# A two-layer decoder trunk: ten low weight parts per layer built by ScalarE and an adding DMA, and queries and keys as one 512-column product

## The chip, the cores and the metric

The kernel runs on one core of one Trainium2 chip. The metric is the device time of one execution in microseconds. The kernel before was run three times; its median is 938.72 us (938.2 to 939.96). With a median of 939 us and runs this close together, about 0.2% (1.9 us) is what a measurement can tell from no change.

## The reference, cut to what is computed

```python
# x: (1, 256, 1024) float32; DEPTH = 2 layers; D_FF = 2816; 4 heads of 64 in each attention
def reference(x, ...):
    for l in range(DEPTH):
        x = x + 0.5 * swiglu(rms_norm(x, ffn1_norm[l]), ffn1_gate[l], ffn1_up[l], ffn1_down[l])
        h = rms_norm(x, mix_norm[l]) @ w_in[l]              # 1024 -> 2304 columns
        u_pool = h[..., :256]                               # pooling
        qm, km, vm = split(h[..., 256:1024], 3)             # block-sparse ("moba") attention
        qd, kd, vd = split(h[..., 1024:1792], 3)            # dilated attention
        u_conv = h[..., 1792:]                              # convolution, 31 taps
        y_pool = pool_mixer(u_pool, pool_w[l], pool_scale[l])
        y_moba = moba_attention(rope(qm), rope(km), vm)
        y_dil  = dilated_attention(rope(qd), rope(kd), vd)
        y_conv = conv_module(u_conv, ...)                   # ends in a layer norm and silu
        x = x + concatenate([y_pool, y_moba, y_dil, y_conv]) @ w_out[l]
        x = x + 0.5 * swiglu(rms_norm(x, ffn2_norm[l]), ffn2_gate[l], ffn2_up[l], ffn2_down[l])
    return rms_norm(x, final_norm)
```

## The kernel before

All matrix products run on TensorE in a 32-bit format of reduced mantissa (fp32r). To keep accuracy, each operand is split in a high part (the value rounded to that format) and a low part (the rest), and each product is the sum of three: high times high, high times low, low times high.

The weights come as a stream of **units** of 128 partitions by up to 2048 columns (1 MB), in the order in which they are used. `prep` loads a unit in two halves of 128x1024: SyncE (SP) issues a DMA into a buffer `raw` (four of them, in turn), ScalarE (ACT) writes the high part `hi` as a copy of `raw`, and VectorE (DVE) writes the low part `lo` as `raw` minus `hi`. `hi` and `lo` are rings of five units, so a unit's buffers are free when the unit five places before it has been used. `raw` is free when both ACT and DVE have read it.

A layer is a first feed-forward part (22 gate/up units `gu`, 16 halves of down units `dn`), the mixing part (9 units `wi` of the input projection, 4 units `wo` of the output projection), and a second feed-forward part. In the mixing part the `wi` units are, in order: conv gate and conv value (`cg`, `ca`), `qd`, `kd`, two for both values `v`, `qm`, `km`, and the pooling columns `pu`. `by_tokens` makes queries and keys: tokens are the stationary side, 256 features of the weights the moving side, so a unit is 48 matmuls of 128x256. The two `v` units hold 512 features per block of 128 inputs and are made by 48 matmuls of 128x512. `rope` scales the product out of PSUM with ACT, rotates with four DVE operations, transposes on TensorE (`tr_qd`, `tr_kd`, ...) and copies the result back with ACT; `scores` and `softmax` follow (`qk_d`, `s_d`, `p_d`), then `pv` transposes the probabilities (`pt_d`), copies them (`pts_d`) and multiplies with `v`. The results are split into `mx` (high by ACT, low by DVE), the operand of the output projection, which takes its four units in the order `W_OUT = (4, 0, 2, 6)`: dilated attention, pooling, moba (`mx` from `pv_m`) and convolution. The 31 convolution taps are mostly DVE operations on `yv`, and a layer norm (`ln`, `rb_ln`) and a silu (`lth`) end them.

Nothing is in the written order: `Plan` records all operations with their dependencies, estimated costs (`rec`) and a due time, and emits them in an order of its own. Every engine then runs its instructions in exactly that order, and waits on semaphores. A changed operation therefore also moves its neighbours.

GpSimd (POOL) only adds the squares for the norms (`acc_f`, `acc_m`).

Of the kernel before, what the change touches and what calls it, by code (L numbers as in the profile page):

```python
# [8 lines left out]
F32 = mybir.dt.float32  # L9
# [7 lines left out]
T = 256  # L17
# [34 lines left out]

ALL, BLOCKS = ((0, KC),), ((0, 4), (4, 6), (6, 7), (7, 8))
W_OUT = (4, 0, 2, 6)

# [15 lines left out]
class View:  # L71
# [21 lines left out]
    def rows(self, n=2):  # L93
        return self._then(lambda t: t.unsqueeze(1).to_broadcast([128, n, T]))

    def heads(self):
        return self._then(lambda t: t.to_broadcast([128, 2, 4, t.shape[3]]))

# [165 lines left out]
def trunk(ctx: ExitStack, tc: tile.TileContext, d):  # L264
# [53 lines left out]
    def dma_act(out, in_):  # L318
        rec("act", 0.47, nc.scalar.dma_start, [out], [], (), {"out": out, "in_": in_}, lat=1.8)

    def store(out, in_, cols):
        rec("sp", max(0.1, cols * 0.00142), nc.sync.dma_start, [], [in_], (), {"out": out, "in_": in_}, lat=0.91)
# [95 lines left out]

    units, output = [], set()
    for l in range(DEPTH):  # L420
        for w in range(2):
            for f in range(FC):
                units.append((d["gu"][l, w, f], 16))
            for m in range(KC):
                for h in range(2):
                    units.append((d["dn"][l, w, m, :, h * HALF:(h + 1) * HALF], FC // 2))
            if w == 0:
                for k in range(9):
                    units.append((d["wi"][l, k], 16))
                for k in range(4):  # L430
                    output.add(len(units))
                    units.append((d["wo"][l, k], 16))
    made = []
# [52 lines left out]
    def prep():  # L486
        n = len(made)
        src, ch = units[n]
        hi = plan.buf(ring, [128, UNIT], F32R, f"hi{n % RING}", f"hi{n}")
        lo = plan.buf(ring, [128, UNIT], F32R, f"lo{n % RING}", f"lo{n}")  # L490
        parts = 2
        plan.lead = LEAD if n in output else 0.0
        where = []
        for i in range(parts):
            a, b = ch * i // parts, ch * (i + 1) // parts
            where += [i] * (b - a)
            a, b = a * 128, b * 128
            raw = plan.buf(ring, [128, UNIT // 2], F32, turn("raw", RAW), f"raw{n}_{i}")[:, :b - a]
            h, o = hi.on(i)[:, a:b], lo.on(i)[:, a:b]
            dma(raw, src[:, a:b], b - a)  # L500
            A(b - a, h, raw, AF.Copy)
            tt(b - a, "tensor_sub", o, raw, h.bitcast(F32))

        plan.lead = 0.0

        def part(c, n=1):

            s = slice(c * 128, (c + n) * 128)
            return hi.on(where[c])[:, s], lo.on(where[c])[:, s]

        made.append(part)
# [212 lines left out]
    def mix(l, nrm, after):  # L724
# [61 lines left out]

        def rope(i, j, nm, col):

            ps = by_tokens(nm)
            q = slot(i, f"{nm}t{l}")  # L790
            for t in range(2):
                A(T, q.on(t)[:, t], ps.on(t)[:, t], AF.Copy, scale=col[:, t:t + 1])
            v = q.rearrange("p t (h e) -> p t h e", h=4)
            a = work("ra", 2, [128, 2, 4, 16], f"ra_{nm}{l}")
            b = work("rb", 2, [128, 2, 4, 16], f"rb_{nm}{l}")
            tt(64, "tensor_mul", b.on(0)[:, :, :, 0:8], v[:, :, :, 8:16], sin_t[:, :, :, 0:8].heads())
            tt(64, "tensor_mul", b.on(1)[:, :, :, 8:16], v[:, :, :, 0:8], sin_t[:, :, :, 8:16].heads())
            tt(128, "tensor_mul", a, v[:, :, :, 0:16], cos_t.heads())
            tt(128, "tensor_add", v[:, :, :, 0:16], a, b)
            ps = bank("qk", 2, [128, 2, T], f"tr_{nm}{l}")  # L800
            for t in range(2):
                for c in range(2):
                    transpose(0.09, ps.on(2 * t + c)[:, c, t * 128:(t + 1) * 128], q[:, t, c * 128:(c + 1) * 128])
            out = slot(j, f"{nm}{l}")
            A(512, out, ps, AF.Copy)
            return out

# [27 lines left out]

        qd = rope(8, 14, "qd", qcol)
        kd = rope(9, 15, "kd", nrm.col)
        pd = [p for c in range(2) for p in scores(qd, kd, c, C_BD, f"d{l}", 16)]


        psv = [bank("mm", 4, [128, 512], f"v{l}{t}") for t in range(2)]
        vt = [flat(slot(20 + t, f"vt{l}{t}")) for t in range(2)]
        sv = [Sum(), Sum()]
        for u in range(2):
            part = take()
            for t in range(2):
                sl = slice(t * 128, (t + 1) * 128)
                for i in range(4):
                    k = u * 4 + i
                    wh, wl = part(4 * i, 4)  # L850
                    xh, xl = nrm.y[k].on(0)[:, 0, sl], nrm.y[k].on(1)[:, 1, sl]
                    sv[t].mm(0.65, psv[t], (xh, wh), (xh, wl), (xl, wh))
        for t in range(2):
# [25 lines left out]

        qm = rope(8, 23, "qm", qcol)  # L880
        km = rope(9, 24, "km", nrm.col)
        pv(pd, 256, 4, 16, f"d{l}")
# [213 lines left out]
```

## Time and profile before

| what | value |
|---|---|
| median of three runs | 938.72 us |
| the profiled execution's own time | 939.43 us |
| its span in the trace | 937.6 us |
| TensorE busy | 924.9 us (99% of the span) |
| VectorE busy | 721.5 us (77%) |
| ScalarE busy | 563.8 us (60%) |
| GpSimd busy | 33.3 us (4%) |
| granted TensorE clock over the span | 0.997 |

The table is to be read with the chain of work that ended last: an engine that is busy for 99% of the span leaves little to gain from the others, except where it waits for them. The span of a profiled execution is 1.83 us shorter than that execution's device time.

### The profile page before, as it was taken

How to read it: one execution, taken by the hardware profiler on the slowest of the kernel's cores; microseconds unless marked ns; L12 is line 12 of the kernel's file. 1: busy time of each engine (PE TensorE's matmuls, PEld its weight loads, DVE VectorE, ACT ScalarE, POOL GpSimd, SP SyncE). 2: the span in 40 equal slices, each digit the busy share in tenths (PEclk: the TensorE clock that was granted, in tenths of full speed). 3: DMA queues.
4: the chain of work that ended last, by engine and by line, in shares of the span. 5: the costliest groups of instructions: out<-in, count | busy, mean ns of one | idle time of the engine just before them, and what ended most of it. 6: DMA issues, size and time to landing. Idle time of an engine off the chain costs nothing.

```text
span 937.6 us, 15074 instructions
## 1 busy us (share of the span) xinstructions
PE 924.9 (99%) x5644; PEld 822.4 (88%) x5644; DVE 721.5 (77%) x1329; ACT 563.8 (60%) x1049; POOL 33.3 (4%) x45
## 2 busy tenths in 40 slices
PE   9999999999999999999999999999999999999996
PEld 8888888898998888888888888888988988888885
DVE  6789976679888988765778887667797888886652
ACT  7776655558576676555546565445667776565540
POOL 0000000100002000000000000011000200000010
PEclk9999999999999999999999999999999999999998
DMA  8856566762164756456765554567512576654641
GB/s 301 280 199 214 171 179 199 232 217 93 35 229 156 249 200 209 127 161 195 251 213 181 180 189 137 166 193 253 187 46 96 197 239 212 221 173 125 187 125 45
DMA packets 55210, 170.18 MB, mean 181 GB/s; under 512 B 6368, under 2 KB 8416, under 8 KB 55136
## 3 DMA queue, kind: packets, MB, share of 16 engines
q1 hardware_dynamic: 54704, 168.92, 55.9%
q8 instruction: 44, 0.72, 0.3%
q10 hardware_dynamic: 432, 0.29, 0.1%
q14 instruction: 30, 0.25, 0.1%
HBM read 168.14 MB, written 1.05 MB: 180 GB/s over the span
## 4 chain that ended last, share of the span: by engine, by line
PE 93%; DVE 3%; DMA 2%; ACT 1%; issue 1%; DVEq 0%; SPq 0%; ACTq 0%
PE mm_gu L368 50%; PE dn L368 26%; PE v L368 2%; PE wo L368 2%; PE pu L368 1%; PE qd L368 1%; PE qm L368 1%; PE kd L368 1%; PE km L368 1%; PE mm_cg L368 1%; PE mm_ca L368 1%; DMA raw<-in_gu_dram 1%; DVE lo L312 1%; DVE y_f L346 1%; DMA x<-in_x_dram 1%
## 5 line engine op out<-in xcount | busy, mean ns | idle before, releaser
L312 DVE TENSOR_TENSOR lo<-raw,hi 128x1024 fp32r<-128x1024 f32 (+3 forms) x365 | 387.7, 1087 | 63.1 <-ACT hi L312 47.3
L312 ACT ACTIVATE hi<-raw 128x1024 fp32r<-128x1024 f32 (+3 forms) x365 | 329.6, 938 | 137.3 <-PE dn L368 54.8
L368 PE MATMUL mm_gu<-y_f,hi 128*128 128x512 f32 x1408 | 332.4, 391 | 0.9 <-DVE y_f L346 0.7
L368 PEld LDWEIGHTS mm_gu<-y_f,hi 128*128 128x128 f32 x1408 | 260.7, 188 | 54.8 <-ACT hi L312 1.8
L368 PEld LDWEIGHTS mm_gu<-y_f,lo 128*128 128x128 f32 x1408 | 176.0, 191 | 4.0
L368 PE MATMUL mm_gu<-y_f,lo 128*128 128x256 f32 x1408 | 178.1, 283 | 0.0
L368 PE MATMUL dn<-h,hi 128*128 128x512 f32 x704 | 169.4, 390 | 0.0
L368 PEld LDWEIGHTS dn<-h,hi 128*128 128x128 f32 x704 | 128.7, 188 | 24.1
L312 DVE TENSOR_TENSOR t<-mm_gu,t 128x256 f32<-128x256 f32 x176 | 73.0, 421 | 49.8 <-ACT t L312 47.1
L368 PEld LDWEIGHTS dn<-h,lo 128*128 128x128 f32 x704 | 91.5, 191 | 4.3
L368 PE MATMUL dn<-h,lo 128*128 128x256 f32 x704 | 92.8, 282 | 0.0
L312 ACT ACTIVATE t<-mm_gu 128x256 f32<-128x256 f32 x176 | 64.3, 375 | 30.0 <-PE mm_gu L368 29.9
L312 ACT ACTIVATE h<-th 128x256 fp32r<-128x256 f32 x88 | 36.4, 417 | 63.2 <-DVE th L312 63.1
L312 DVE TENSOR_TENSOR t<-t,rb_f 128x512 f32<-128x512 f32 x88 | 60.2, 686 | 0.9
L312 ACT ACTIVATE th<-t 128x256 f32<-128x256 f32 x88 | 36.5, 415 | 40.3 <-DVE t L312 28.5
L346 DVE SCALAR_TENSOR_TENSOR x<-dn,x 128x256 f32<-128x256 f32 x64 | 27.0, 422 | 38.8 <-PE dn L368 38.2
L368 PE MATMUL wo<-mx,hi 128*128 128x256 f32 x256 | 48.4, 289 | 1.7 <-DVE mx L312 1.7
L346 DVE SCALAR_TENSOR_TENSOR yv<-hpad,par,yv 128x256 f32<-128x256 f32 x108 | 44.0, 478 | 0.0
L312 DVE TENSOR_TENSOR h<-th,h 128x256 fp32r<-128x256 f32 x88 | 36.8, 420 | 7.6 <-ACT h L312 6.8
L368 PEld LDWEIGHTS wo<-mx,hi 128*128 128x128 f32 x256 | 39.9, 191 | 2.3 <-DVE mx L312 2.2
L312 DVE TENSOR_TENSOR th<-th,t 128x256 f32<-128x256 f32 x88 | 36.8, 419 | 5.5 <-ACT th L312 5.1
L368 PE MATMUL wo<-mx,lo 128*128 128x256 f32 x128 | 36.2, 283 | 0.0
(209 smaller groups left out, 674.4 us busy)
## 6 DMA issues: line engine op xcount, KB each, us to landing
raw<-in_gu_dram SPq DMA_DIRECT2D x170, 512.0 KB, 4.5
raw<-in_dn_dram SPq DMA_DIRECT2D x64, 384.0 KB, 3.6
raw<-in_dn_dram SPq DMA_DIRECT2D x64, 320.0 KB, 3.0
raw<-in_wi_dram SPq DMA_DIRECT2D x36, 512.0 KB, 4.7
raw<-in_wo_dram SPq DMA_DIRECT2D x16, 512.0 KB, 3.9
raw<-in_gu_dram SPq DMA_DIRECT2D x9, 256.0 KB, 5.5
con<-in_con_dram SPq DMA_DIRECT2D x1, 932.0 KB, 7.5
x<-in_x_dram SPq DMA_DIRECT2D x3, 256.0 KB, 5.4
```

The lines of the kernel that those rows point to most:

```text
L312: f(*[val(x) for x in a], **{n: val(x) for n, x in k.items()})
L346: nc.vector.scalar_tensor_tensor(out, in0=a, scalar=scalar, in1=b, op0=op0, op1=op1)
L368: nc.tensor.matmul(val(o), lhsT=val(lhsT), rhs=val(rhs), start=self.i == 0, stop=self.i == self.n - 1, skip_group_check=True)
```

## The change

Two edits. First, for five units of each layer (the ninth `wi` unit, which holds the pooling columns, and the four `wo` units) the low part is no longer a DVE subtraction: ACT writes minus the high part into `lo`, and a DMA issued by GpSimd adds the weights from DRAM onto it. Second, queries and keys of one attention are one product of 512 features: their columns lie side by side in the two units, and the function `wide`, which `v` uses too, runs through both units for both halves of the tokens. `rope` then works on one half of the tokens at a time, queries and keys together.

```diff
@@
+APART = (8,)
@@
+    def dma_add(out, in_):
+        rec("pool", 1.2, nc.gpsimd.dma_start, [out], [], (), {"out": out, "in_": in_, "accum_op": ALU.add}, lat=5.0)
@@
                 for k in range(9):
+                    if k in APART:
+                        apart.add(len(units))
                     units.append((d["wi"][l, k], 16))
                 for k in range(4):
                     output.add(len(units))
+                    apart.add(len(units))
                     units.append((d["wo"][l, k], 16))
@@
             A(b - a, h, raw, AF.Copy)
-            tt(b - a, "tensor_sub", o, raw, h.bitcast(F32))
+            if n in apart:
+                A(b - a, o, h.bitcast(F32), AF.Copy, scale=-1.0)
+                dma_add(o, src[:, a:b])
+            else:
+                tt(b - a, "tensor_sub", o, raw, h.bitcast(F32))
@@
-        def rope(i, j, nm, col):
-
-            ps = by_tokens(nm)
-            q = slot(i, f"{nm}t{l}")
+        def wide(nm):
+
+            ps = [bank("mm", 4, [128, 512], f"{nm}{l}{t}") for t in range(2)]
+            sm = [Sum(), Sum()]
+            for u in range(2):
+                part = take()
+                for t in range(2):
+                    sl = slice(t * 128, (t + 1) * 128)
+                    for i in range(4):
+                        y = nrm.y[u * 4 + i]
+                        wh, wl = part(4 * i, 4)
+                        xh, xl = y.on(0)[:, 0, sl], y.on(1)[:, 1, sl]
+                        sm[t].mm(0.68, ps[t], (xh, wh), (xh, wl), (xl, wh))
+            return ps
+
+        def rope(i, j, nm):
+
+            ps = wide(f"qk{nm}")
+            out = [bank("qk", 2, [128, 2, T], f"tr_{n}{nm}{l}") for n in "qk"]
             for t in range(2):
-                A(T, q.on(t)[:, t], ps.on(t)[:, t], AF.Copy, scale=col[:, t:t + 1])
...
-            for t in range(2):
-                for c in range(2):
-                    transpose(0.09, ps.on(2 * t + c)[:, c, t * 128:(t + 1) * 128], q[:, t, c * 128:(c + 1) * 128])
-            out = slot(j, f"{nm}{l}")
-            A(512, out, ps, AF.Copy)
-            return out
+                qk = flat(slot(i + t, f"qk{nm}t{l}{t}"))
+                for n, col in enumerate((qcol, nrm.col)):
+                    s = slice(n * T, (n + 1) * T)
+                    A(T, qk.on(n)[:, s], ps[t][:, s], AF.Copy, scale=col[:, t:t + 1])
...
+                tt(64, "tensor_mul", b.on(0)[:, :, 0:8], v[:, :, 8:16], sin[:, :, 0:8].to_broadcast([128, 8, 8]))
+                tt(64, "tensor_mul", b.on(1)[:, :, 8:16], v[:, :, 0:8], sin[:, :, 8:16].to_broadcast([128, 8, 8]))
+                tt(128, "tensor_mul", a, v[:, :, 0:16], cos.to_broadcast([128, 8, 16]))
+                tt(128, "tensor_add", v[:, :, 0:16], a, b)
+                for n in range(2):
+                    for c in range(2):
+                        f = n * T + c * 128
+                        transpose(0.09, out[n].on(2 * t + c)[:, c, t * 128:(t + 1) * 128], qk[:, f:f + 128])
+            res = []
+            for n in range(2):
+                res.append(slot(j + n, f"{'qk'[n]}{nm}{l}"))
+                A(512, res[n], out[n], AF.Copy)
+            return res
@@
-        qd = rope(8, 14, "qd", qcol)
-        kd = rope(9, 15, "kd", nrm.col)
+        qd, kd = rope(8, 14, "d")
@@
-        qm = rope(8, 23, "qm", qcol)
-        km = rope(9, 24, "km", nrm.col)
+        qm, km = rope(8, 23, "m")
```

The host code lays the weight columns out to match. The order of SP's DMA issues does not change. At three places the order moves as follows.

TensorE, layer 0, in the values' product behind the dilated queries and keys (`v`: the values; `tr_kd`, `tr_qd`: transposes of the rotated keys and queries; `qk_d`: the scores). Before:

```order
L368 MATMUL v_2391<-hi_2098,y_m_3_1844 128x512
L312 MATMUL tr_kd_2422<-ident,kdt_2395 128x128 x4
L368 MATMUL v_2427<-hi_2098,y_m_0_1624 128x512
L368 MATMUL v_2427<-lo_2125,y_m_0_1624 128x512
L368 MATMUL v_2427<-hi_2098,y_m_0_1624 128x512
L368 MATMUL v_2427<-hi_2098,y_m_1_1696 128x512
L368 MATMUL v_2427<-lo_2125,y_m_1_1696 128x512
L368 MATMUL v_2427<-hi_2098,y_m_1_1696 128x512
L380 MATMUL qk_d_2437<-kd_2431,qd_2346 128x128
```

and with the change:

```order
L311 MATMUL tr_qd_2325<-ident,qkdt_2328 128x128 x2
L311 MATMUL tr_kd_2330<-ident,qkdt_2328 128x128 x2
L370 MATMUL v_2333<-hi_2098,y_m_3_1844 128x512
L370 MATMUL v_2333<-lo_2125,y_m_3_1844 128x512
L370 MATMUL v_2333<-hi_2098,y_m_3_1844 128x512
L370 MATMUL v_2368<-hi_2098,y_m_0_1624 128x512
L370 MATMUL v_2368<-lo_2125,y_m_0_1624 128x512
L370 MATMUL v_2368<-hi_2098,y_m_0_1624 128x512
L382 MATMUL qk_d_2374<-kd_2366,qd_2361 128x128
```

Between the last transposes and the scores there are six matmuls of `v` in both; before, those transposes were of the keys alone, now they are of both.

ScalarE, layer 0, from the layer norm's squares (`lsq`) to the high parts of the moba result (`mx` from `pv_m`). Before:

```order
L312 ACTIVATE lsq_2993<-yv_2354 128x512
L312 ACTIVATE hi_3008<-raw_0_2843 128x1024
L312 ACTIVATE hi_3008<-raw_1_2919 128x1024
L312 ACTIVATE hi_3021<-raw_0_2949 128x1024
L312 ACTIVATE hi_3021<-raw_1_2988 128x1024
L312 ACTIVATE mx_3052<-pv_m_2998 128x256
L312 ACTIVATE mx_3059<-pv_m_3003 128x256
L312 ACTIVATE rb_ln_3071<-ln_3015 128x256
```

and with the change:

```order
L311 ACTIVATE lsq_2910<-yv_2338 128x512
L311 ACTIVATE lo_2925<-hi_2701 128x1024 x2
L311 ACTIVATE hi_2937<-raw_0_2611 128x1024
L311 ACTIVATE hi_2937<-raw_1_2639 128x1024
L311 ACTIVATE lo_2969<-hi_2937 128x1024 x2
L311 ACTIVATE rb_ln_2995<-ln_2931 128x256
L311 ACTIVATE mx_3000<-pv_m_2915 128x256
L311 ACTIVATE mx_3007<-pv_m_2920 128x256
```

The third output unit (`lo_2925`) now has its negation here, behind it comes the fourth (`hi_2937`, `lo_2969`); six operations of 128x1024 instead of four, and `rb_ln`, stand ahead of `mx`.

VectorE at the same place, from the end of the layer norm's iteration (`y_ln`) to the low parts of the moba result. Before:

```order
L346 SCALAR_TENSOR_TENSOR y_ln_3028<-a_ln_3033,y_ln_3028 128x2
L312 TENSOR_TENSOR lo_3013<-raw_1_2919,hi_3008 128x1024
L312 TENSOR_TENSOR lo_3076<-raw_0_2949,hi_3021 128x1024
L312 TENSOR_TENSOR yv_2354<-yv_2354,rb_ln_3071 128x512
L312 TENSOR_TENSOR lo_3076<-raw_1_2988,hi_3021 128x1024
L312 TENSOR_TENSOR mx_3052<-pv_m_2998,mx_3052 128x256
L312 TENSOR_TENSOR mx_3059<-pv_m_3003,mx_3059 128x256
```

and with the change:

```order
L348 SCALAR_TENSOR_TENSOR y_ln_2944<-a_ln_2946,y_ln_2944 128x2
L311 TENSOR_TENSOR yv_2338<-yv_2338,rb_ln_2995 128x512
L311 TENSOR_TENSOR mx_3000<-pv_m_2915,mx_3000 128x256
L311 TENSOR_TENSOR mx_3007<-pv_m_2920,mx_3007 128x256
L348 SCALAR_TENSOR_TENSOR yv_2338<-lth_3025,yv_2338 128x512
```

The three low parts that stood between the iteration and `mx` are gone from VectorE.

## Rows read from the trace of the kernel before

**Rows 1.** The page: busy time of each engine, then the chain's shares by engine
```profile
PE 924.9 (99%) x5644; PEld 822.4 (88%) x5644; DVE 721.5 (77%) x1329; ACT 563.8 (60%) x1049; POOL 33.3 (4%) x45
...
PE 93%; DVE 3%; DMA 2%; ACT 1%; issue 1%; DVEq 0%; SPq 0%; ACTq 0%
```

**Rows 2.** Waits of TensorE: what waited for what, us in total, times, longest
```profile
PE wo L368 <- DVE mx L312: 1.7, 2, 0.9
...
PE mm_gu L368 <- DVE y_f L346: 0.7, 2, 0.4
PE st_f L312 <- DVE y_f L346: 0.4, 1, 0.4
```

**Rows 3.** Timeline of TensorE: start, us, operation, xcount; narrow keys, then wide values
```profile
213.95 0.28 PE L368 MATMUL kd<-lo,y_m 128*128 128x256 f32 x1
...
214.67 0.28 PE L368 MATMUL kd<-lo,y_m 128*128 128x256 f32 x1
...
215.15 0.40 PE L368 MATMUL v<-lo,y_m 128*128 128x512 f32 x1
...
217.21 0.39 PE L368 MATMUL v<-lo,y_m 128*128 128x512 f32 x1
```

**Rows 4.** Timeline of TensorE: the same values' product, later
```profile
223.22 0.39 PE L368 MATMUL v<-lo,y_m 128*128 128x512 f32 x1
...
225.30 0.39 PE L368 MATMUL v<-lo,y_m 128*128 128x512 f32 x1
...
225.98 0.39 PE L368 MATMUL v<-lo,y_m 128*128 128x512 f32 x1
...
228.02 0.39 PE L368 MATMUL v<-lo,y_m 128*128 128x512 f32 x1
```

**Rows 5.** Timeline: ScalarE's copy of the keys, TensorE's first scores
```profile
218.30 0.60 ACT L312 ACTIVATE kd<-tr_kd 128x512 f32<-128x512 f32 x1
...
219.59 0.93 PE L380 MATMUL qk_d<-kd,qd 64*128 64x128 f32 x8
```

**Rows 6.** Timeline of TensorE: the third output unit, which holds the moba result
```profile
269.50 0.28 PE L368 MATMUL wo<-mx,hi 128*128 128x256 f32 x1
270.65 0.38 PE L368 MATMUL wo<-mx,hi 128*128 128x256 f32 x1 [0.87 <-DVE mx L312]
```

**Rows 7.** Timeline of ScalarE ahead of that unit
```profile
261.38 0.62 ACT L312 ACTIVATE lsq<-yv 128x512 f32<-128x512 f32 x1
261.91 3.89 ACT L312 ACTIVATE hi<-raw 128x1024 fp32r<-128x1024 f32 x4
...
267.17 0.39 ACT L312 ACTIVATE rb_ln<-ln 128x256 f32<-128x256 f32 x1 [0.83 <-PE ln L312]
```

**Rows 8.** Timeline of VectorE ahead of that unit
```profile
268.44 0.68 DVE L312 TENSOR_TENSOR yv<-yv,rb_ln 128x512 f32<-128x512 f32 x1
269.04 1.22 DVE L312 TENSOR_TENSOR lo<-raw,hi 128x1024 fp32r<-128x1024 f32 x1
270.18 0.75 DVE L312 TENSOR_TENSOR mx<-pv_m,mx 128x256 fp32r<-128x256 f32 x2
```

**Rows 9.** Groups by line and shape, 191 to 285 us: xcount, busy us, mean ns
```profile
L312 DVE TENSOR_TENSOR lo<-raw,hi 128x1024 fp32r<-128x1024 f32 x23 | 27.7, 1220 | 2.4 <-ACT hi L312 2.4
...
L312 ACT ACTIVATE hi<-raw 128x1024 fp32r<-128x1024 f32 x24 | 24.3, 1055 | 6.6 <-issue 3.1 <-DMA raw<-in_gu_dram 2.8 <-PE dn L368 0.5
```

**Rows 10.** SP's nine loads of 512 KB, 262 to 285 us: issue to landing
```profile
DMA to landing us min/median/max: 3.2/4.9/6.1
```

**Rows 11.** Stretches: us, busy PE, PEld, DVE, ACT, POOL, clock, DMA share, GB/s
```profile
234.00:240.00 6.00, 6.00 (x53) 6.00 (x52) 5.54 (x17) 1.44 (x3) 0.00 (x0) 1.00 0.00 0
240.00:247.00 7.00, 7.00 (x65) 6.58 (x66) 6.83 (x20) 3.46 (x8) 0.00 (x0) 1.00 0.00 0
...
270.00:276.00 6.00, 5.35 (x44) 5.35 (x45) 5.49 (x9) 4.27 (x7) 0.00 (x0) 1.00 0.81 274
```

**Rows 12.** The chain that ended last, layer 0, into the second feed-forward part
```profile
290.81 6.21 DMA raw<-in_gu_dram
297.05 1.06 ACT hi L312
```

More of the change, by code (lines that the diff above doesn't have):

```diff
@@ L94, in rows @@
         return self._then(lambda t: t.unsqueeze(1).to_broadcast([128, n, T]))
-    def heads(self):
-        return self._then(lambda t: t.to_broadcast([128, 2, 4, t.shape[3]]))
     def to_broadcast(self, shape):
@@ L416, in trunk @@
         Sum().mm(0.4, warm[:, 0:128], (mean_w, mean_w))
-    units, output = [], set()
+    units, output, apart = [], set(), set()
     for l in range(DEPTH):
@@ L785, in by_tokens @@
             return ps
-        def rope(i, j, nm, col):
-            ps = by_tokens(nm)
-            q = slot(i, f"{nm}t{l}")
-            for t in range(2):
-                A(T, q.on(t)[:, t], ps.on(t)[:, t], AF.Copy, scale=col[:, t:t + 1])
[L793 to L800, printed above, removed]
-            for t in range(2):
-                for c in range(2):
-                    transpose(0.09, ps.on(2 * t + c)[:, c, t * 128:(t + 1) * 128], q[:, t, c * 128:(c + 1) * 128])
-            out = slot(j, f"{nm}{l}")
-            A(512, out, ps, AF.Copy)
-            return out
+        def wide(nm):
[11 more added lines that the diff above has]
+            return ps
@@ new lines, in rope @@
+        def rope(i, j, nm):
+            ps = wide(f"qk{nm}")
+            out = [bank("qk", 2, [128, 2, T], f"tr_{n}{nm}{l}") for n in "qk"]
+            for t in range(2):
+                qk = flat(slot(i + t, f"qk{nm}t{l}{t}"))
+                for n, col in enumerate((qcol, nrm.col)):
+                    s = slice(n * T, (n + 1) * T)
+                    A(T, qk.on(n)[:, s], ps[t][:, s], AF.Copy, scale=col[:, t:t + 1])
+                v = qk.rearrange("p (h e) -> p h e", h=8)
+                a = work("ra", 2, [128, 8, 16], f"ra_{nm}{l}{t}")
+                b = work("rb", 2, [128, 8, 16], f"rb_{nm}{l}{t}")
+                sin, cos = sin_t[:, t], cos_t[:, t]
+                tt(64, "tensor_mul", b.on(0)[:, :, 0:8], v[:, :, 8:16], sin[:, :, 0:8].to_broadcast([128, 8, 8]))
[11 more added lines that the diff above has]
+            return res
@@ L834, in softmax @@
             return p
-        qd = rope(8, 14, "qd", qcol)
-        kd = rope(9, 15, "kd", nrm.col)
+        qd, kd = rope(8, 14, "d")
         pd = [p for c in range(2) for p in scores(qd, kd, c, C_BD, f"d{l}", 16)]
-        psv = [bank("mm", 4, [128, 512], f"v{l}{t}") for t in range(2)]
+        psv = wide("v")
         vt = [flat(slot(20 + t, f"vt{l}{t}")) for t in range(2)]
[L843 to L852, printed above, removed]
         for t in range(2):
@@ L1053 @@
     plw = np.zeros((DEPTH, 128, 2, 128), f32)
-    cols = [16, 17, 14, 15, 8, 9, 10, 11, 2, 3, 4, 5, 0, 1]
+    cols = [16, 17, 14, 15, 0, 1]
     for l in range(DEPTH):
@@ L1060 @@
         win = I["w_in"][l].reshape(KC, 128, 18, 128)
-        wi[l, [0, 1, 2, 3, 6, 7, 8]] = (win[:, :, cols].reshape(KC, 128, 7, 2, 128).transpose(2, 1, 0, 3, 4)
-                                        .reshape(7, 128, UNIT))
-        wi[l, 4:6] = win[:, :, [6, 7, 12, 13]].reshape(2, 4, 128, 512).transpose(0, 2, 1, 3).reshape(2, 128, UNIT)
+        wi[l, [0, 1, 8]] = (win[:, :, cols].reshape(KC, 128, 3, 2, 128).transpose(2, 1, 0, 3, 4)
+                            .reshape(3, 128, UNIT))
+        for u, four in ((2, [8, 9, 10, 11]), (4, [6, 7, 12, 13]), (6, [2, 3, 4, 5])):
+            wi[l, u:u + 2] = win[:, :, four].reshape(2, 4, 128, 512).transpose(0, 2, 1, 3).reshape(2, 128, UNIT)
         wot = I["w_out"][l].reshape(KC, 128, KC, 128)
```

## The prediction

> **What bounds the kernel now.** I read the page first, then the waits of TensorE, then the timeline at each place where it waits. TensorE is busy for 924.9 of 937.6 us and carries 93% of the chain that ended last [rows 1]. So only two things can shorten this kernel by more than a trifle: fewer or cheaper columns on TensorE, or one of its few waits taken away. VectorE at 77% and ScalarE at 60% [rows 1] hide behind it nearly everywhere, and what an edit takes from them is worth only what TensorE waited for it. Those waits are few [rows 2]: 1.7 us in two pieces, one per layer, for the low part of the moba result (`mx`) in the third output unit, 0.7 us in two pieces for `y_f` and 0.4 us for the row transposes of the norm behind the output projection. One of the 0.7 us's two pieces lies at the kernel's start, which the change doesn't touch; the other, 0.4 us, and the last one are in layer 0 behind the mixing part. So 1.75 + 0.8 = 2.55 us is all that a relieved VectorE can give here.
>
> **The change part by part.**
>
> *Wide queries and keys.* Removed per attention: 96 matmuls of 128x256; added: 48 of 128x512. Columns are the same, so the difference is what each instruction costs beside its columns. The narrow ones start every 0.120 us: six between 213.95 and 214.67 [rows 3]. The wide ones of `v`, which have the very form of the new ones, start every 0.229 us: nine between 215.15 and 217.21 [rows 3]. A pair of narrow ones costs 0.240, so each wide one saves 0.011 us, 48 of them 0.53 us, and four attentions (two in each layer) 2.1 us. The later stretches of the same product bound it: nine in 2.08 us give 0.2311 and 1.7 us, nine in 2.04 us give 0.2267 and 2.55 us [rows 4]. All of it is on TensorE and so on the path. I take 2.1, the stretch nearest to the place of the new products. ScalarE's copies out of PSUM and VectorE's four rotations keep number and size, as do the transposes.
>
> *The new order around the scores.* Before, queries were transposed and copied long before the keys. Now the last transposes bring both, and ScalarE has two copies of 128x512 to make where it had one, under the same six matmuls of `v` (6 x 0.229 = 1.37 us). Before, the keys' copy ended at 218.90 and the scores began at 219.59 [rows 5]: 0.69 us to spare. The second copy takes a further 0.5 to 0.6 of it, if ScalarE is free at once. That leaves about 0.1 us, and nothing if a convolution tap stands ahead of the copies. Bounds: 0, if all fits; if both attentions in both layers lose half a copy more, 4 x 0.35 = 1.4 us. I take +0.4.
>
> *VectorE's share of the low parts.* Removed: ten subtractions in each layer at 1.22 us, 24.4 us in all [rows 9]. Added on ScalarE: as many negations, priced as the copy of the same shape, 1.055 us or 0.97 apart when four run in a row (3.89/4) [rows 7, 9], some 20 us. Both are beside TensorE's work except at one place. In the third output unit TensorE stood from its first matmul at 269.50 until 270.65 [rows 6], because the low part of `mx` came at 270.18 on VectorE behind a low part of 1.22 us at 269.04 [rows 8]. Both layers do this. With the change three of those low parts are no longer there, but ScalarE has more ahead of `mx`: from the end of `lsq` at about 261.9 [rows 7] six operations of 0.97 end at 267.7, `rb_ln` (0.3) at 268.0, the first high part of `mx` at 268.35. VectorE multiplies `yv` meanwhile (0.6, to 268.6) and has the first low part at 269.0; with some 0.2 us to TensorE it comes at 269.2, where the second matmul of the unit would start at 269.62. So the wait goes, with 0.4 us to spare: the price that ScalarE pays stays under cover, but just so. Bounds 0 and 1.75 us; I take 1.5. (All of these times move earlier together by what the wide products save ahead of them; distances stay.)
>
> *The feed-forward part behind it, layer 0.* The 0.4 us wait for the norm's row hangs on a load that was issued at 290.81 and took 6.2 us [rows 12]: `raw` had come free late, since a VectorE that ran behind had still to read it. For the ten halves `raw` is now free when ScalarE has read it, so the next loads leave earlier, into a DMA that stood idle from 234 to 247 us [rows 11]. Between 0 and 0.8 us; I take half, 0.4.
>
> *The adding DMA.* Ten in a layer, 512 KB each, issued by GpSimd, whose queue holds nothing else there; behind them are only its additions for the next norm, which wait for the finished output projection anyway. They use DRAM reads that the DMA has room for [rows 11], but the low part now exists only when the transfer has landed. No row shows a transfer from GpSimd, nor one that adds. Where TensorE needs the data late this doesn't matter: the pooling unit and the first two output units are negated far ahead. The third output unit is the tight one. Its first negation ends at 261.9 + 0.97 = 262.9, its low part is wanted by the unit's third matmul at 269.74: 6.9 us. The fourth unit's negations end near 266.7 and 267.7 and are wanted at 275.3 and 275.6: 8 us or more. The nearest rows are SP's loads of the same size in this stretch: 3.2 to 6.1 us, median 4.9 [rows 10]. With ScalarE's signal and GpSimd's issue ahead of it, 5 to 7 us would fit. The upper bound is two such transfers in one, since the destination is read as well: 9.8 by the median, 12.2 by the longest. I take about 7, at the edge, and put +0.2 us a layer on it: 0.4.
>
> The Trainium skill, DMA: Bandwidth & Descriptors, section Anatomy of one DMA — SWDGE (gpsimd) path, gives 2.0 us plus the bytes over 436 GB/s for a plain transfer from this queue; as an estimate that is 3.2 us for 512 KB, and by it the term would be nothing. SP's row is longer than that for a plain load, and no run here shows GpSimd's.
>
> *Sum,* against the profiled execution: 939.43 - 2.1 + 0.4 - 1.5 - 0.4 + 0.4 = 936.2 us. That execution was 0.7 us over the median of the three runs, 938.72, so against the median the same sum of -3.2 gives **935.5 us**.
>
> **The rivals.**
>
> *1. The additions land late, and the third output unit waits longer than before.* At 9.8 us from the negation's end the low part comes at 272.7, TensorE waits 2.95 instead of 0.87 us, 2.1 more in each layer: 4.2 - 2.1 (wide) = +2.1, 940.8 us. At 12.2 it is 275.1, a wait of 5.3, 4.5 more in each layer: 8.9 - 2.1 = +6.8, 945.5 us. The fourth unit then finds its own landed. It decides from 8.8 us on (the wide products' gain is spent) and is slower by more than 0.2% from 9.7 us. For it: two reads for one write, and a DMA that was 81% busy at 270 to 276 [rows 11]. Against it: the loads that filled it then leave earlier now. The Trainium skill, Collectives: The Full Stack, section The bandwidth ceiling: the fold count and why AG ≠ RS ≠ AR, has this as a rule: a transfer that adds reads two sources through one ring and ran at half the rate of a copy there. No run here shows it yet. Chance 0.17; a landing between 8 and 9.7 us, which ends within 0.2% (about 938.5), 0.08.
>
> *2. The products gain and the new order takes it back.* If `rope`'s copies are late in all four attentions (+1.4), the `mx` wait stays by half (ScalarE's six operations late by the 0.4 us that are to spare, and more), and layer 0's waits stay: -2.1 + 1.4 - 0.9 = -1.6, about 937.1 us, no measurable change. For it: margins of 0.1 and 0.4 us. Chance 0.16.
>
> *3. The wide product is no cheaper than two narrow ones.* If the new ones start every 0.24 us, only the waits are left: -1.5, 937.2 us. Against it stand all three stretches of `v`. Chance 0.02.
>
> **How the numbers follow.** Forecast, with everything between a gain of 1.9 and of 5.1 us (all of the wide products at their best and all waits): 0.57. Faster by over 0.2% (1.9 us, about what a measurement of this kernel can tell from no change) is that case alone, 0.57. Within 0.2%: 0.16 + 0.02 + 0.08 = 0.26. Slower: 0.17. The low end of the range is 938.72 - 5.1 = 933.6, less half a microsecond for the spread of the runs, 933.1; the high end goes into rival 1 as far as a landing of about 10.5 us (+3.4), 942.1, and leaves out some 0.1 above.
>
> **What the profile of the changed kernel would show.** Step 1: the product of queries and keys at 0.227 to 0.231 us from start to start, four products some 2 us shorter in all. Step 2: no wait of TensorE ahead of `qk_d` and `qk_m` above 0.4 us. Step 3: no wait of the output product for `mx`. Step 4: no wait for `y_f` in layer 0 behind the mixing part. Step 5: GpSimd's transfers at 5 to 7 us from issue to landing; a wait of the output product for a DMA, and its length, is the measure of rival 1. The prediction is wrong if that wait is over 2 us a layer, or if the queries' and keys' copies have become what the scores wait for.

## The result: 950.38 us, and the profile after

The changed kernel takes 950.38 us (median of four runs, 948.25 to 951.54) against 938.8 us for the kernel before beside it: a ratio of 1.0118 with a 95% interval of 1.0106 to 1.0131. It is slower by some 11 us where 3 us of gain were forecast. The profiled execution took 950.8 us, its span is 948.9 us.

The page of the changed kernel: busy time of each engine, the chain's shares, the DMA queues (packets, MB, share of 16 engines' span; q1 carries SP's loads, q0 GpSimd's transfers), and three kinds of DMA with their median time to landing:

```profile
PE 926.3 (98%) x5452; PEld 816.0 (86%) x5452; DVE 699.4 (74%) x1309; ACT 582.4 (61%) x1069; POOL 49.4 (5%) x65
...
q1 hardware_dynamic: 54704, 168.92, 55.0%
q0 software_dynamic: 2880, 10.49, 5.9%
...
PE 86%; DMA 8%; ACT 3%; DVE 1%; issue 1%; ACTq 0%; DVEq 0%; SPq 0%
...
raw<-in_wo_dram SPq DMA_DIRECT2D x16, 512.0 KB, 8.7
lo<-in_wo_dram POOLq DMA_DIRECT2D x16, 512.0 KB, 11.9
```

Against [rows 1], VectorE lost 22 us of work and ScalarE took on 19, as reckoned, and TensorE's share of the chain fell from 93 to 86%: what came in is DMA, 8% where it was 2. The waits of TensorE in the changed kernel (us in total, times, longest):

```profile
PE wo L370 <- DMA lo<-in_wo_dram: 9.9, 4, 2.7
PE st_f L311 <- DVE y_f L348: 1.6, 1, 1.6
...
PE pt_d L311 <- ACT pts_d L311: 0.8, 1, 0.8
```

The `mx` waits of [rows 2] are gone, and layer 0's waits for `y_f` behind the mixing part too. In their place the output product waits 9.9 us for adding transfers. (The 1.6 us for `y_f` lie in the first feed-forward part, which the change doesn't touch: in the profiles of the sixteen kernels told of here the queries' product of layer 0 starts between 202.6 and 203.9 us, here at 203.9. The 0.8 us for `pts_d` lie in layer 1.) The places, in TensorE's timeline of layer 0 (start, us):

```profile
270.32 0.28 PE L370 MATMUL wo<-mx,lo 128*128 128x256 f32 x1
...
274.10 0.58 PE L370 MATMUL wo<-mx,lo 128*128 128x256 f32 x1 [2.54 <-DMA lo<-in_wo_dram]
...
277.46 0.31 PE L370 MATMUL wo<-mx,lo 128*128 128x256 f32 x1
...
282.64 0.38 PE L370 MATMUL wo<-mx,lo 128*128 128x256 f32 x1 [2.13 <-DMA lo<-in_wo_dram]
```

The third unit runs through its first half and stops at the second, the fourth does the same. GpSimd issues the four transfers of these units at 263.47, 264.4, 267.26 and 268.2; the time from issue to landing is 5.3, 9.6, 10.6 and 14.4 us (GpSimd's timeline):

```profile
263.47 1.81 POOL L311 DMA_DIRECT2D lo<-in_wo_dram  x2 [17.14 <-ACT lo L311]
267.26 1.81 POOL L311 DMA_DIRECT2D lo<-in_wo_dram  x2 [1.98 <-PE ln L311]
```

and, in the view of the tile, the shortest, median and longest of each pair:

```profile
DMA to landing us min/median/max: 5.3/7.5/9.6
...
DMA to landing us min/median/max: 10.6/12.5/14.4
```

So they land at 268.8, 274.0, 277.9 and 282.6: one by one, 3.9 to 5.2 us apart, and two of the four are the ends of TensorE's two waits. Stretches of the changed kernel (columns as in [rows 11]):

```profile
234.00:240.00 6.00, 6.00 (x28) 4.75 (x27) 5.97 (x18) 5.29 (x8) 2.36 (x3) 1.00 0.95 214
240.00:247.00 7.00, 7.00 (x62) 6.56 (x63) 6.83 (x20) 6.87 (x12) 1.73 (x2) 1.00 1.05 273
...
270.00:276.00 6.00, 3.46 (x23) 3.26 (x22) 4.30 (x6) 4.22 (x7) 0.00 (x0) 0.84 1.02 242
```

The DMA, idle here before (0.00 in both of the first two stretches of [rows 11]), is now full: the first six transfers fill it from 234 us on, the last four meet SP's loads for the feed-forward part.

Where the time lies, from the starts of the first and last matmuls of the tiles in TensorE's timeline, us for layer 0 / layer 1 (two of the kernels below beside it):

| kernel | queries' product to end of `v` | on to the last `wo` | on to the last gate/up |
|---|---|---|---|
| before | 25.6 / 25.6 | 53.8 / 53.8 | 124.6 / 123.1 |
| changed | 25.0 / 25.0 | 58.9 / 61.7 | 123.0 / 122.9 |
| changed, transfers not issued | 25.0 / 25.0 | 52.1 / 52.1 | 123.0 / 122.9 |
| changed, first six transfers only | 25.0 / 25.0 | 52.1 / 52.3 | 123.2 / 123.0 |

The two outer stages gain, 0.6 us a layer in the first, 1.7 in layer 0's feed-forward part; the stage with the transfers loses 5.1 and 7.9 us.

### The profile page after: what moved, and what is told of

Read it like the earlier page. It is cut to its first block, busy times and chain, and to the rows that moved or that the text cites. A ratio compares the mean times of both kernels' runs of the same rounds, so it can differ in the third digit from the quotient of the medians.

```text
span 948.9 us, 14742 instructions
## 1 busy us (share of the span) xinstructions
PE 926.3 (98%) x5452; PEld 816.0 (86%) x5452; DVE 699.4 (74%) x1309; ACT 582.4 (61%) x1069; POOL 49.4 (5%) x65
## 3 DMA queue, kind: packets, MB, share of 16 engines
q0 software_dynamic: 2880, 10.49, 5.9%
## 4 chain that ended last, share of the span: by engine, by line
PE 86%; DMA 8%; ACT 3%; DVE 1%; issue 1%; ACTq 0%; DVEq 0%; SPq 0%
PE mm_gu L370 47%; PE dn L370 26%; DMA lo<-in_wo_dram 3%; DMA raw<-in_gu_dram 3%; PE wo L370 2%; PE qkd L370 2%; PE v L370 1%; PE mm_cg L370 1%; PE pu L370 1%; PE mm_ca L370 1%; PE qkm L370 1%; ACT hi L311 1%; DMA x<-in_x_dram 1%; DMA raw<-in_wo_dram 1%; ACT lo L311 1%
## 5 line engine op out<-in xcount | busy, mean ns | idle before, releaser
L311 DVE TENSOR_TENSOR lo<-raw,hi 128x1024 fp32r<-128x1024 f32 (+3 forms) x345 | 363.0, 1077 | 65.8 <-ACT hi L311 50.2
L370 PE MATMUL wo<-mx,hi 128*128 128x256 f32 x256 | 51.6, 302 | 0.0
L370 PE MATMUL wo<-mx,lo 128*128 128x256 f32 x128 | 38.7, 303 | 9.9 <-DMA lo<-in_wo_dram 9.9
L370 PEld LDWEIGHTS wo<-mx,hi 128*128 128x128 f32 x256 | 43.0, 207 | 0.3 <-issue 0.3
```

The lines of the kernel that those rows point to most:

```text
L311: f(*[val(x) for x in a], **{n: val(x) for n, x in k.items()})
L370: nc.tensor.matmul(val(o), lhsT=val(lhsT), rhs=val(rhs), start=self.i == 0, stop=self.i == self.n - 1, skip_group_check=True)
```

## Experiments

### What of the transfers costs

Three kernels leave all engines in the changed kernel's order and change the transfers alone. None at all:

```diff
-        rec("pool", 1.2, nc.gpsimd.dma_start, [out], [], (), {"out": out, "in_": in_, "accum_op": ALU.add}, lat=5.0)
+        rec("pool", 1.2, lambda **k: None, [out], [], (), {"out": out, "in_": in_}, lat=5.0)
```

> The changed kernel, every engine in the same order, but the ten adding transfers of a layer are not issued (so in five units of each layer the low part holds minus the high part, and the weights are not added). Theory A, the loss of 11.6 us is the transfers alone, late for the output product and crowding the DMA: 934 to 937 us, no wait of the output product for a DMA, no loads over 7 us there. Theory C, ScalarE's twenty negations and the new order around the moba result cost it: 945 us or more, with a wait of the output product for ScalarE or VectorE. Between the two, 940 to 944, each has a part.

Measured 934.05 us, ratio 0.995 (0.9935 to 0.9964). Theory A: the whole loss is the transfers', and a gain of 5.1 us stands behind it. The only wait of TensorE that this profile shows between the program's first and last steps stands at 8.6 us, in the first feed-forward part; from there to the last norm there is none:

```profile
PE mm_gu L370 <- DVE lo L311: 0.5, 1, 0.5
```

Then the same transfers as plain copies:

```diff
-{"out": out, "in_": in_, "accum_op": ALU.add}
+{"out": out, "in_": in_}
```

> The changed kernel, every engine in the same order, but GpSimd's transfers write the weights over the low part where the changed kernel adds them onto it (so in five units of each layer the low part holds the whole weight). Theory A1, it is the adding (the destination is read too): a transfer alone lands in about 3 to 5 us, a line of four moves at 2 to 3 us apiece, the wait of the output product falls from 9.9 us to under 2, and the time is 936 to 941 us. Theory D, it is GpSimd's queue, whatever it carries: a line still moves at 4 us or more apiece, 947 to 952 us.

Measured 936.72 us (0.9979, 0.997 to 0.9988), waits of the output product for a DMA 2.1 us. So of the 16.3 us between the kernels with and without transfers, 13.7 go with the adding and 2.7 with the copying. And the adding transfer with half the columns:

```diff
-{"out": out, "in_": in_, "accum_op": ALU.add}
+{"out": out[:, 0:512], "in_": in_[:, 0:512], "accum_op": ALU.add}
```

> The changed kernel, every engine in the same order, each of the ten adding transfers of a layer carrying the first 512 of its 1024 columns (the other half of those low parts holds minus the high part, the weights are not added there). Theory bytes, the line goes by what is moved: 2 to 2.5 us from landing to landing where it was 4.3 to 5.3, the waits of the output product for a DMA fall from 9.9 us to under 1, 934 to 937 us. Theory count, each transfer costs by itself: 4 us and more from landing to landing, waits of 6 us or more, 944 us or more.

Measured 936.11 us (0.9961, 0.9948 to 0.9973), waits 1.8 us; the time is theory bytes', the waits a little more than it said. What the two have in common stands in the queue line of the page, of the plain copies:

```profile
q0 software_dynamic: 2880, 10.49, 3.2%
```

and of the half adding transfers:

```profile
q0 software_dynamic: 2880, 5.24, 3.3%
```

Adding 5.24 MB keeps the DMA engines about as long as copying 10.49 MB; adding 10.49 MB took 5.9% (the page of the changed kernel above), 1.84 times the plain copies. The number of transfers is the same in all three. The line is not bytes alone, though: in layer 0 of all three kernels the second of the four late transfers lands 5.2 to 5.7 us behind the first, and two loads of SP are issued in between (265.1 and 266.0 us in the changed kernel); the third and fourth follow 2.5 and 1.2 us later as plain copies, 3.9 and 4.7 as additions.

### Which of the ten

Only the third and fourth output unit by adding transfer, the other six low parts by VectorE again (`APART` empty, and ahead of the output units' `apart.add` a condition):

```diff
+                    if k in (2, 3):
                         apart.add(len(units))
```

> The changed kernel with only the third and fourth output unit by negation and adding transfer (four transfers in a layer where it had ten, the other six low parts by VectorE again). Theory A, the line of four begun at 263 is the loss: the waits for a DMA stay at 8 to 11 us, and with what VectorE loses 948 to 954 us. Theory E, the six early transfers cause it: those waits fall under 4 us, 940 to 946 us.

Measured 956.72 us (1.0194, 1.017 to 1.0218), waits for a DMA 9.8 us: theory A in the waits, and 2.7 us above its range in the time, with waits for VectorE and ScalarE beside them (2.4 us of `pt_m` for `yv`, 1.7 of `psp` for `pl`) that the wide product alone has too (next section). Four transfers with none ahead of them form the same line. GpSimd's timeline, and TensorE's where it waits:

```profile
266.22 1.01 POOL L311 DMA_DIRECT2D lo<-in_wo_dram  x1 [79.56 <-DVE yv L311]
267.91 0.87 POOL L311 DMA_DIRECT2D lo<-in_wo_dram  x1 [0.68 <-PE ln L370]
270.74 1.81 POOL L311 DMA_DIRECT2D lo<-in_wo_dram  x2 [1.96 <-ACT lo L311]
...
277.45 0.39 PE L370 MATMUL wo<-mx,lo 128*128 128x256 f32 x1 [2.12 <-DMA lo<-in_wo_dram]
...
285.96 0.58 PE L370 MATMUL wo<-mx,lo 128*128 128x256 f32 x1 [3.57 <-DMA lo<-in_wo_dram]
```

Its transfers landed 7.4, 9.5, 10.5 and 14.2 us after issue. And the complement, the pooling unit and the first two output units by transfer, the last two by VectorE:

```diff
+                    if k in (0, 1):
                         apart.add(len(units))
```

> The changed kernel with the pooling unit and the first two output units by adding transfer (six in a layer, none late for its use), the third and fourth output unit by VectorE's subtraction. The complement of the kernel with these two alone (956.7 us). If only the late four hurt: no wait of the output product for a DMA, some of VectorE's wait ahead of the moba result back (1.7 us), 935 to 940 us. If the six early ones hurt by filling the DMA: 942 us or more, with waits for hi or raw.

Measured 934.92 us, ratio 0.9954 (0.9939 to 0.9968): faster than both kernels. Its six transfers took 8.4 to 14.8 us each and nobody waited for one; the line is there, and it is done before its use. VectorE, with three units' subtractions less, has the other four low parts and `mx` in time; TensorE's only waits between the program's first and last steps are 1.2 us of gate/up for a high part and 0.3 for a norm, all in the first feed-forward part, which the change doesn't touch.

### Each edit alone

The wide product alone (no unit is put in `apart`):

```diff
-APART = (8,)
+APART = ()
...
+                    if k in ():
                         apart.add(len(units))
```

> Queries and keys as one product of 512 features, all low parts by VectorE as before. Theory A, the loss is the transfers' and the wide product gains as forecast: 936 to 938 us (-2.1 for the product, 0 to +0.4 for the order around the scores; the wait for the low part of the moba result stays, 1.7 us). Theory B, the wide product's order costs more than it gains (rival 2 taken further): 940 us or more, with waits ahead of qk_d and qk_m.

And the transfers alone, the first edit made in the kernel before:

```diff
+            if n in apart:
+                A(b - a, o, h.bitcast(F32), AF.Copy, scale=-1.0)
+                dma_add(o, src[:, a:b])
+            else:
                 tt(b - a, "tensor_sub", o, raw, h.bitcast(F32))
```

> The kernel before with the ten low parts of a layer by negation and adding transfer, narrow products kept. Theory A: the loss of the changed kernel and the 2 us that the wide product gives, 951 to 954 us, waits of the output product for a DMA of 8 to 11 us in all. Theory B, the two edits together cause the loss (the shorter products in front leave the transfers less time): 940 to 946 us.

Measured 945.8 us (1.0081, 1.0064 to 1.0097) and 939.63 us (1.0009, 1.0 to 1.0018). Both expectations of theory A fell. Theory B of the first has the time (940 us or more) and not the place, that of the second is missed by 0.4 us. The wide product alone loses 6.7 us, though its own stage is 0.6 us a layer shorter. The transfers alone neither lose nor gain clear of the noise, and no wait for them is in that profile (an execution of 941.58 us, the slowest of ten): its stage up to the last `wo` is 1 us a layer shorter than before, and its gate/up part some 2 us a layer longer (with 1.9 us of waits for `y_f` there, and in layer 0 the granted clock at 0.52 from 284.0 to 287.5 us). The waits of the kernel with the wide product alone:

```profile
PE pt_m L311 <- DVE yv L348: 2.4, 2, 1.2
PE psp L370 <- ACT pl L311: 1.7, 2, 0.8
PE ln L370 <- DVE lsq L311: 1.6, 2, 1.2
PE wo L370 <- DVE lo L311: 1.6, 2, 0.8
PE mm_gu L370 <- ACT hi L311: 1.6, 3, 0.9
```

None stands ahead of the scores. They come from further up. A stretch (columns as in [rows 11]) of the kernel before:

```profile
216.00:229.00 13.00, 13.00 (x70) 9.91 (x69) 11.78 (x41) 11.53 (x31) 0.00 (x0) 1.00 0.29 103
```

and of the wide product alone:

```profile
216.00:229.00 13.00, 13.00 (x67) 9.87 (x66) 9.15 (x37) 12.68 (x37) 0.00 (x0) 1.00 0.01 3
```

The DMA stands still for 13 us and VectorE is idle for 3.9 of them, while ScalarE has no time left. What it does not do there is the pooling unit's high parts. ScalarE's timeline in the kernel before:

```profile
216.24 2.00 ACT L312 ACTIVATE hi<-raw 128x1024 fp32r<-128x1024 f32 x2
```

and with the wide product alone:

```profile
228.42 1.05 ACT L311 ACTIVATE hi<-raw 128x1024 fp32r<-128x1024 f32 x1
```

Before, ScalarE made five of the convolution's gates (`gt`) while TensorE was still busy with the keys, and was through with the sixth at 216.4 us. With queries and keys together it waits 0.7 and 1.9 us for the halves of the product, copies both out of PSUM at 212.1 and 214.9 us, makes all six gates behind that, and the planner puts the pooling unit behind the dilated softmax, 12 us later. Until ScalarE has read that unit `raw` isn't free, so SP can't load, and VectorE has its low parts to make later, in the middle of the convolution's taps. In the changed kernel the same shift moves the transfers: the first leaves at 231.7 us, with the narrow product at 220.1, and the third unit's leave at 263.5 instead of 243.6 and 245.8 (GpSimd's timelines). That was tested by moving the unit's due time, in the kernel with the wide product alone and in the changed kernel (`ninth` holds the pooling unit's number; in the changed kernel `apart` stands there, which picks the same unit, since the others in it are in `output`):

```diff
-        plan.lead = LEAD if n in output else 0.0
+        plan.lead = LEAD if n in output else 30.0 if n in ninth else 0.0
```

> Queries and keys as one product, all low parts by VectorE (945.8 us so), and the pooling unit's preparation due 30 us earlier. Theory A2, the loss of that kernel too is the displaced preparation (weights stand still from 216 to 229 us, convolution and low parts pile up on VectorE behind it): 936 to 940 us, its waits of 7 to 8 us for yv, pl, lsq and lo mostly gone. Theory V, VectorE lacks the time in the wide order wherever that unit stands: 943 to 947 us.

> The changed kernel, with the due time of the pooling unit's preparation 30 us earlier in the planner, so that ScalarE makes its two high parts and negations ahead of the dilated softmax, as the kernel with narrow products and adding transfers does, and the units behind it follow some 11 us earlier. Theory A2, the wide product pushes ScalarE's preparation of the pooling unit behind the softmax, and the transfers are late by that shift alone: 935 to 938 us, waits of the output product for a DMA under 1.5 us in all. Theory A, ten adding transfers of 4.5 us are too slow for this stage wherever they begin: 945 us or more.

Measured 939.43 us (0.9999, 0.999 to 1.0008), 6.4 us back, and 940.65 us (1.0018, 1.0008 to 1.0027), 9.7 us back; the high parts stand at 215.0 and 215.4 us. In the second no wait for a DMA is left at the output product, with the third unit's transfers leaving at 249.31:

```profile
219.74 1.92 POOL L311 DMA_DIRECT2D lo<-in_wi_dram  x2 [32.15 <-ACT lo L311]
...
249.31 1.80 POOL L311 DMA_DIRECT2D lo<-in_wo_dram  x2 [6.00 <-ACT lo L311]
```

Theory A2 holds for the shift, but the second kernel is 2.7 us above its range. Whether the transfers cost those:

> The changed kernel with the pooling unit prepared early (940.65 us so), every engine in that order, and the ten adding transfers of a layer not issued (five units' low parts hold minus the high part; the weights are not added). Theory A2 with E: the 6 us by which that kernel stays behind the one without transfers (934.05) are still the transfers', which fill the DMA and delay the loads of the next feed-forward part: 933 to 936 us, no wait of mm_gu for hi or y_f over 0.5 us. Theory O: they are the order's: 938 to 941 us.

Measured 938.62 us (0.9997, 0.9989 to 1.0006): theory O. In that order the transfers cost 2.0 us, no more; that it stays 4.6 us behind the same work in the changed kernel's order is the order's (in the two profiled executions, whose spans are 6.0 us apart, 1.1 and 0.8 us up to the last `wo` and 2.1 and 1.8 in the gate/up part). Which of its places costs that was not tried. The three orders side by side, us:

| order | low parts by VectorE | negated, no transfer | negated, with transfers |
|---|---|---|---|
| narrow products | 939.1 | not run | 939.6 |
| wide | 945.8 | 934.05 | 950.4 |
| wide, pooling unit early | 939.4 | 938.6 | 940.65 |

The second and third columns of a row are one order with and without the transfers, which cost 16.3 and 2.0 us. For the first column the planner had made the order anew, so the 11.8 us (second row) and 0.8 (third) between it and the next are the worth of the subtractions and of that order together.

### Other choices

The planner told that an adding transfer takes 20 us, which moves the third unit's negations ahead of `lsq`:

```diff
-"accum_op": ALU.add}, lat=5.0)
+"accum_op": ALU.add}, lat=20.0)
```

> The changed kernel, with an adding transfer taken as 20 us long in the planner where it was 5: the third output unit's two negations move from behind the layer norm's squares to some 8 us ahead of them, all else nearly as it was. Theory A, four transfers in one line at 4 to 5 us each, begun at 263: the line is now two and two, no wait of the output product for a DMA above 0.5 us, 934 to 938 us. Theory E, the six transfers before them fill the DMA and that delays what follows: a wait of 4 us or more stays, 941 us or more.

Measured 953.42 us (1.0145, 1.0128 to 1.0163). No wait of the output product for a DMA, as theory A has it, and yet slower: the order around it moved as well, and TensorE waits for `pts_d` (3.5 us), `yv` (2.5), `mn_m` (1.6) and `y_f` (3.4) instead. As a test of the time it is inconclusive.

In the order with the pooling unit early, the transfers for the first two output units alone, for the first three, and for the pooling unit and the first three (the three lines, one for each kernel; the first two with `APART` empty):

```diff
+                    if k in (0, 1):
...
+                    if k in (0, 1, 2):
...
+                    if k in (0, 1, 2):
```

> Wide queries and keys, the pooling unit prepared early with VectorE's subtraction, and negation and adding transfer for the first two output units alone (four transfers in a layer, from about 233 to 246 us, where the DMA stood idle, VectorE was full and ScalarE had room). If the transfers cost only where they meet the loads or a late use: 935 to 938 us, no wait of the output product for a DMA, psp and y_f waits about halved from 3.4 us. If any adding transfers cost by themselves: 940 us or more.

> The same with the third output unit too (six transfers in a layer). Its two transfers start near 246 and land near 256 to 260, ten microseconds ahead of their use: if only lateness and meeting the loads matter, 934.5 to 938 us and VectorE's wait ahead of the moba result gone. If crowding starts with the loads of the fourth unit: 0.5 to 2 us slower than with two.

> The changed kernel with the pooling unit early (940.65 us so) and the fourth output unit's two transfers, issued at 265 to 267 us into the loads of the feed-forward part, replaced by VectorE's subtractions. If those two are what is left of the transfers' price there (about 2 us): 937 to 939 us, no wait of mm_gu for hi. If the order is what is left: 940 to 942 us.

Measured 942.65 us (1.0039, 1.0025 to 1.0053), 937.53 us (0.9984, 0.9975 to 0.9993) and 940.64 us (1.001, 1.0001 to 1.002). The second is in its range, though a wait of 0.8 us for `mx` is left. The third is in its second range (the order), but it doesn't part the two: against the kernel that it starts from, TensorE's waits in the feed-forward parts behind the mixing fell from 2.6 us to none, and those for `mx` rose from 0.5 to 2.6, as VectorE now makes the subtractions. What the fourth unit's transfers cost by themselves stays open; without any transfer that order has 2.0 us of the first kind. The first came out above 940 us, through a load and not through a low part. Its chain of waits in the profiled execution (the slowest of six, 944.77 us):

```profile
236.24 13.72 DMA raw<-in_wo_dram
249.96 0.02 issue
249.98 1.06 ACT hi L311
251.04 0.28 ACT mx L311
251.32 0.02 issue
251.34 0.44 DVE mx L311
251.78 0.04 issue
251.82 0.92 PE qk_m L382 x4
```

A load of SP, issued into the four adding transfers, took 13.7 us; its high part stood ahead of `mx` in ScalarE's queue, and TensorE stood with it for 1.9 us. In the changed kernel SP's loads from 229 to 262 us take 11.5 us in the median, in the same order without transfers 4.3 (shortest, median, longest, in this order):

```profile
DMA to landing us min/median/max: 3.7/11.5/14.6
...
DMA to landing us min/median/max: 3.1/4.3/5.2
```

With the first six transfers alone they take 8.1, the longest 15.0, and nothing is lost by it. In these kernels it mattered whether something urgent was queued behind the load's reader, and not how long the load took.

## Why the prediction was wrong, step by step

*Step 1 (wide pace) was right.* In the changed kernel's product the triple of matmuls at 209.41 us and the one at 214.84 are eight triples apart:

```profile
209.41 0.62 PE L370 MATMUL qkd<-hi,y_m 128*128 128x512 f32 x2
...
214.84 0.39 PE L370 MATMUL qkd<-hi,y_m 128*128 128x512 f32 x1
```

24 starts in 5.43 us are 0.226 us each, the good end of what [rows 3, 4] gave.

*Step 2 (order around the scores) was right on the scores and wrong as a price of the order.* No wait stands ahead of `qk_d` or `qk_m`. But the step followed the two copies as far as the scores and not what was queued behind them on ScalarE: the pooling unit's high parts, now behind the softmax, were not weighed. Steps 1 and 2 by themselves sum to -1.7 us (-2.1 + 0.4); the wide product alone measured +6.7. With step 1 right, the order costs some 8.8 us there and not 0.4. Where VectorE is relieved and no transfer issued, none of it shows.

*Steps 3 and 4 (VectorE's relief) were right in sign, step 4 too small.* The `mx` wait and layer 0's `y_f` waits are gone, and the gate/up part of layer 0 fell by 1.7 us where 0.4 were forecast and 0.8 was the bound; what the other 0.9 us are was not traced. ScalarE's times ahead of `mx` came within 0.2 us of the forecast:

```profile
262.12 1.99 ACT L311 ACTIVATE lo<-hi 128x1024 fp32r<-128x1024 f32 x2
...
268.07 0.65 ACT L311 ACTIVATE mx<-pv_m 128x256 fp32r<-128x256 f32 x2
```

Steps 1 to 4 together, measured by the kernel without transfers, are -5.1 us; the sum said -3.6 without the transfers' term, and the low end of its range -5.1.

*Step 5 (the adding DMA) failed.* Its term was +0.4 us and measured 16.3. The first of the late four lands in 5.3 us, as forecast, and the third unit's first half was in time. The step priced one transfer by itself, and of the third unit only the first half. Four leave within 5 us, and they go one behind another through DMA engines that SP's loads want too. That there was room was read from [rows 11], stretches of a kernel without the transfers; ten additions at 1.84 times a copy's engine time fill the room themselves. As an estimate from the page, 5.9% of 948.9 us for 20 additions is 2.8 us of all 16 engines for each, 11 us for a line of four, beside SP's loads.

*Rival 1 had the mechanism, at half its size.* Its 9.8 us from the negation's end are what the third unit's second half took (9.9 us, from its negation's end at 264.1 to 274.0), and its wait is 2.54 us, near the 2.95 given. But "the fourth unit then finds its own landed" was wrong: that unit waits 2.13 us, and in layer 1 the longest wait, 2.7 us, is its own. And a further price was in no term: behind three of the four waits TensorE runs slow. Stretches of the output product in the changed kernel, two of layer 0 and two of layer 1:

```profile
274.00:277.50 3.50, 3.40 (x16) 3.40 (x17) 0.00 (x0) 0.51 1.06 268
277.50:280.50 3.00, 3.00 (x25) 2.81 (x24) 0.00 (x0) 1.00 1.04 274
...
738.30:741.70 3.40, 2.88 (x13) 2.88 (x14) 0.00 (x0) 0.50 1.07 277
748.50:752.00 3.50, 3.50 (x19) 3.50 (x19) 1.15 (x4) 0.51 0.31 128
```

From 274.10 to 277.46 us the granted clock is the lower of the two levels (0.51), and 15 matmuls take 3.36 us, 0.22 each instead of 0.12: 1.6 us. Waits and this give 6.2 of the 6.8 us that layer 0's stage has more than without transfers. In layer 1 the clock is at the lower level behind both waits, 2.9 us by the same reckoning, which with the two waits (2.54 and 2.74) and that of 0.8 for `pts_d` gives 8.9 of its 9.6. Rival 1's upper bound, two loads in one, was a bound for one addition and not for a line of four, so its chance of 0.17 was too small as well.

The Trainium skill, Collectives: The Full Stack, section The bandwidth ceiling: the fold count and why AG ≠ RS ≠ AR, has a transfer that adds at half the rate of a copy (62.28 to 32.35, 1.93 times). This case agrees with 1.84 times. The Trainium skill, DMA: Bandwidth & Descriptors, section Issuing engines are not separate DMA queues, says that DMAs of all issuers run on the same engines and interleave. SP's loads at 11.5 us instead of 4.3 agree. The same page of the Trainium skill, section Anatomy of one DMA — SWDGE (gpsimd) path, has the formula by which the term would have been nothing (an estimate of 3.2 us). It agrees with the shortest landing of a plain copy, 3.4 us, and not with an addition's, 5.3.

## What to carry to other kernels

A transfer that is priced alone is not priced: count how many are issued within one transfer's time, multiply by what each holds of the DMA engines, and ask when the last half lands; additions belong where their use is a whole line away (the kernel with the first six alone is 0.5% faster than the one before). An edit that brings two results at once can leave the waiting engine in peace and still push the next unit's preparation behind a softmax: follow the queue of the engine that makes the copies, not only the consumer. And where two edits meet, measure each alone: 6.7 and 0.5 us made 11.6 together, and one part of one with the other gave a gain.

## What the runs showed of the hardware

An adding transfer of 512 KB holds the DMA engines 1.84 times as long as a plain one from the same queue and lands 5.3 us after issue as the first of the late four, a plain one 3.4 (as the first of the early six, with loads of SP in flight, 8.3 and 6.3); GpSimd itself is held 0.86 us by each issue where a plain copy takes it 0.53. TensorE's granted clock fell to the lower level behind a wait of 2.54 us and stayed there for 3.4 us of work; behind the one of 2.13 us, 5 us later, it did not. The length of the wait alone does not tell the cases apart: in layer 1 of the kernel with the last four transfers alone it fell behind one of 2.10 us.
